# Four transformer layers: the residual in DRAM during the gate and up products, its tiles for the sums of weights

## The chip, the cores and the metric

One core of a Trainium2 chip. The metric is the device time of one execution in microseconds (us). Before: 2397.15 us, the median of 3 runs (2391.97 to 2398.90).

## The reference

Two blocks of two layers each, on 512 tokens of width 1024 in float32. Each layer is a mixer (several kinds of attention, convolution, gating), a projection back to the residual, and a feed-forward part of width 2816 with a gate. Cut to what the change touches:

```python
def first_block(x, ...):                 # layers 0 and 1
    for layer in range(2):
        mix = mixer(x, ...)
        x = layer_norm(ALPHA * x + mix, ln1_g, ln1_b)
        ffn = (silu(x @ w_gate) * (x @ w_up)) @ w_down
        x = layer_norm(ALPHA * x + ffn, ln2_g, ln2_b)

def second_block(x, ...):                # layers 2 and 3
    for l in range(2):
        x = x + rms_norm(mixer(rms_norm(x), ...) @ w_out, post)
        g, u = split(causal_dwconv(rms_norm(x) @ w_up, cw, cb), 2)
        x = x + rms_norm((gelu(g) * u) @ w_down, fpost)
```

In the feed-forward part the residual x is needed twice: normalized or as it is for the gate and up products, and again after the down product.

## The kernel before, in words

Tokens lie in four tiles of 128. The residual is four tiles `x` of 128 x 1024 float32. Every weight block of 512 KB is fetched by SyncE's queue into a tile `wraw` (three buffers) and split into a high part `whi` (ScalarE, line 248) and a low part `wlo` (VectorE, line 249). A product of a block is then three matmuls for each pair of parts, on TensorE (line 287).

The gate and up products of a layer (`quartered`, from line 514) run over 11 pieces u, each with four weight blocks b11, b12, b21, b22. For each piece the scheme makes seven products instead of eight, q1 to q7, of 24 matmuls each. Three of them take a block as it is: q1 takes b11, q2 takes b21, q3 takes b22. The other four take sums of blocks: q7 takes b12 + b22, q6 takes that + b11, q4 takes that + b21, q5 takes b11 + b12. The first three of these share one tile, `x` of the piece (tile `wsum`, three buffers), which grows from product to product; q5's sum lies in `t1` (tile `rope` or `m`, which hold gains of the normalization before and after).

Sums come about in two ways. GpSimd issues a transfer that adds a block from DRAM to the tile (line 632, 128 of them, and line 625, 8). VectorE adds two tiles (line 617 for t1 from piece 2 on, and line 630 for the last piece's q4: 40 in all). An addition to `wsum` can start only when the product before it has been split, for it changes the tile.

From piece 3 on the products come in the order q7(u), q4(u-1), q3(u-1), q6(u), q2(u), q5(u), q1(u+1); the code's order and the tiles' buffers set the order of work. The first pieces are mixed with the end of the out projection and the normalization: `add_norm` (layers 0 and 1) or `post` and `pre` (layers 2 and 3) finish one token tile after the other, and a function that waits in `self.later` turns each ("the crossing": transposes and sums of the operand's parts). Layers 0 and 1 finish a piece with silu and a multiplication (`gated`); layers 2 and 3 with a short convolution and gelu (`convolved`), which gives VectorE more work. After the products, `out_proj` makes the down product; it reads 22 weight blocks and then normalizes into the tiles `x`.

Of the kernel before, what the change touches and what calls it, by code (L numbers as in the profile page):

```python
# [9 lines left out]
F32 = mybir.dt.float32  # L10
F32R = mybir.dt.float32r
AF = mybir.ActivationFunctionType
ALU = mybir.AluOpType
# [3 lines left out]
P = 128  # L17
# [175 lines left out]
class Kernel:  # L193
# [58 lines left out]
            nc.vector.scalar_tensor_tensor(lo, src, scale, hi.bitcast(F32), op0=ALU.mult, op1=ALU.subtract)  # L252

    def raw(self):
        return self.tl("wraw", [P, 1024], F32, 3)

    def halves(self, place):

# [256 lines left out]
    def quartered(self, l, ops):  # L515
# [4 lines left out]

        nc, w = self.nc, self.t[f"up{l}"]
        room = self.room
        more = [self.piece() for _ in range(4)]
        at = lambda f: room[:, f] if f < 14 else more[f // 2 - 7][:, f % 2]
        sub = nc.vector.tensor_sub
        fc = self.small(f"fc{l}") if l >= 2 else None
        last = KF // 2 - 1

        def block(u, i, j):
            return w[u, i - 1, j - 1].rearrange("p g k c -> p (g k c)")
# [78 lines left out]
        def sums(u):  # L611

            s = st[u]
            s["x"] = load(u, 1, 2, self.tl("wsum", [P, 1024], F32, 3))
            if u > 1:
                first(u)
                nc.vector.tensor_tensor(s["t1"], s["b11"], s["x"], op=ALU.add)

        def first(u):

            s = st[u]
            s["t1"] = self.tl("rope" if u % 2 else "m", [P, D])
            if u < 2:
                load(u, 1, 2, s["t1"])
                nc.gpsimd.dma_start(s["t1"], block(u, 1, 1), accum_op=ALU.add)

        def added(u, i, j):
            x = st[u]["x"]
            if u == last and (i, j) == (2, 1):
                nc.vector.tensor_tensor(x, x, st[u]["b21"], op=ALU.add)  # L630
                return x
            nc.gpsimd.dma_start(x, block(u, i, j), accum_op=ALU.add)  # L632
            return x

        def q7(u):
            s = st[u]
            x = added(u, 2, 2) if u > 1 else s["x"]
            s["c"] = self.bank("tp")
            product(s["c"], x, 4, True)

        def q6(u):
            s = st[u]
# [19 lines left out]
            finish(2 * u, 1, None, (s["c"], s["m"]))  # L662

        sums(0)
        added(0, 2, 2)
        q1(0)
        sums(1)
        added(1, 2, 2)
        q2(0)
        q1(1)  # L670
        while self.later:
            self.behind(self.later.pop(0))
        q2(1)
        first(0)
        first(1)
        q1(2)
        q2(2)
        for f in (q7, 0), (q6, 0), (q7, 1), (q5, 0), (q6, 1), (q4, 0), (q5, 1), (q3, 0):
            f[0](f[1])
        for u in range(2, last + 1):  # L680
            if u == 2:
                sums(2)
            q7(u)
            q4(u - 1)
            q3(u - 1)
            q6(u)
            if u == 2:
                q1(3)
                sums(3)
                q5(2)  # L690
                continue
            q2(u)
            q5(u)
            if u < last:
                q1(u + 1)
                sums(u + 1)
        q3(last)
        q4(last)
        return at
# [668 lines left out]
    def add_norm(self, xs, l, which, nxt):  # L1368

        nc = self.nc  # L1370
        g, b = self.row(f"ln{which}_g", l, "rope"), self.row(f"ln{which}_b", l, "m")
        new = []

        def use(i, ps):
            v = xs[i]
            st = self.tl("lst", [P, 8], F32, 3)
            for j in range(2):
                h = slice(512 * j, 512 * j + 512)
                nc.vector.scalar_tensor_tensor(v[:, h], v[:, h], ALPHA, ps[j], op0=ALU.mult, op1=ALU.add,
                                               accum_out=st[:, j:j + 1])  # L1380
            nc.vector.tensor_scalar(st[:, 2:3], st[:, 0:1], st[:, 1:2], -1.0 / D, op0=ALU.add, op1=ALU.mult)
            nc.vector.tensor_scalar(st[:, 3:4], st[:, 2:3], 1.0 / 32, None, op0=ALU.mult)
            for j in range(2):
                junk = self.tl("rt", [P, S], F32, 2)
                nc.scalar.activation(junk, v[:, 512 * j:512 * j + 512], AF.Square, scale=1.0 / 32, bias=st[:, 3:4],  # L1385
                                     accum_out=st[:, 4 + j:5 + j])
            nc.vector.tensor_scalar(st[:, 6:7], st[:, 4:5], st[:, 5:6], LN_EPS, op0=ALU.add, op1=ALU.add)
            nc.gpsimd.tensor_tensor(st[:, 7:8], st[:, 6:7], self.mhalf[:, 0:1], op=ALU.pow)
            nc.vector.scalar_tensor_tensor(v, v, st[:, 2:3], g, op0=ALU.add, op1=ALU.mult)
            nc.vector.scalar_tensor_tensor(v, v, st[:, 7:8], b, op0=ALU.mult, op1=ALU.add)  # L1390
            new.append(v)
            return nxt(i, v)

        return use, new

    def pre(self, name, then, tag="m"):

# [17 lines left out]

        return use

    def post(self, xs, name, nxt, part=None):

        nc = self.nc  # L1420
        g = self.row(name, 0, "rope")

        def use(i, ps):
            yg = [self.tl("kf", [P, S], F32, 3) for _ in range(2)]
            cols = [slice(512 * j, 512 * j + 512) for j in range(2)]
            st = self.rstd(ps, lambda j: nc.vector.tensor_tensor(yg[j], ps[j], g[:, cols[j]], op=ALU.mult))
            for j, c in enumerate(cols):
                nc.vector.scalar_tensor_tensor(xs[i][:, c], yg[j], st[:, 3:4], xs[i][:, c], op0=ALU.mult, op1=ALU.add)
                if part:
                    part(i, xs[i], c)  # L1430
            return nxt(i, xs[i]) if nxt else None

        return use
# [5 lines left out]
    def run(self):  # L1439
        nc, t = self.nc, self.t  # L1440
        xt = self.parts()
        self.room = self.tl("room_a", [P, 14, S])
        raw = self.room[:, 0:8]

        idle = self.room[:, 13, 0:256]
        nc.vector.memset(idle, 0.0)
        ps = self.bank("sc")
        for _ in range(3):
            self.mm(ps[:, 0:256], idle[:, 0:P], idle)

        def start(k):
            steps = 1 if k else 2
            for i in range(steps):
                c = slice(i * S // steps, (i + 1) * S // steps)
                nc.sync.dma_start(raw[:, k, c], t["xT"][:, k, c])
                self.split(xt[0][:, k, c], xt[1][:, k, c], raw[:, k, c])

        self.start = start
        for l in range(2):
            y, order = self.mixer_a(xt) if l == 0 else self.mixer_c(xt)  # L1460
            if l == 0:
                xs = [self.tl("x", [P, D], F32, 4) for _ in range(NT)]
                for i in range(NT):
                    nc.sync.dma_start(xs[i], t["x"][P * i:P * i + P])
            ops = self.operands()
            use, new = self.add_norm(xs, l, 1, lambda i, v: lambda: self.crossed(v, i, ops))
            self.out_proj(lambda k: y[:, k], KD, t["a_out" if l == 0 else "c_out"], use, order, ops["parts"])
            xs = new
            if self.layers == l + 0.5:
                return [self.store(i, xs[i]) for i in range(NT)]  # L1470
            at = self.quartered(l, ops)
            xt = self.parts()
            last = self.layers == l + 1
            if l == 0:
                nxt = lambda i, v: lambda: self.transposed(v, i, xt)
            else:
                self.load_const("swap", "cmp_mask", "cmp_any", "pool_cnt")
                nxt = self.pre("pre2", lambda v, i: self.transposed(v, i, xt), "kf")
            use, new = self.add_norm(xs, l, 2, self.store if last else nxt)
            self.out_proj(at, KF, t[f"down{l}"], use, DOWN)  # L1480
            xs = new
            if last:
                return
        for l in (2, 3):
            y, order = self.mixer_n(xt, l)
            ops = self.operands()
            use = self.post(xs, f"post{l}", self.pre(f"fpre{l}", lambda v, i: self.crossed(v, i, ops)))
            self.out_proj(lambda k: y[:, k], KD, t[f"out{l}"], use, order, ops["parts"])
            if self.layers == l + 0.5:
                return [self.store(i, xs[i]) for i in range(NT)]  # L1490
            at = self.quartered(l, ops)
            last = self.layers == l + 1
            xt = None if last else self.parts()
            nxt = None if last else self.pre(f"pre{l + 1}", lambda v, i: self.transposed(v, i, xt))
            use = self.post(xs, f"fpost{l}", nxt, self.store if last else None)
            self.out_proj(at, KF, t[f"down{l}"], use, DOWN)
            if last:
                return
# [20 lines left out]
```

## Time and profile before

| | before |
|---|---|
| median of 3 runs | 2397.15 us (2391.97 to 2398.90) |
| the profiled execution | 2403.45 us, its span 2401.5 us |
| TensorE busy | 2284.9 us, 95% |
| VectorE busy | 1490.5 us, 62% |
| ScalarE busy | 1162.3 us, 48% |
| GpSimd busy | 187.1 us, 8% |
| mean granted TensorE clock | 0.979 of full speed |
| read from DRAM | 292.21 MB |

The profile is of one execution on the core's engines. A row's idle time is the time just before it in which its engine did nothing, with what ended it. The chain that ended last is followed back from the last instruction: each step is a piece of work or a transfer that released the next. The granted clock is what TensorE was allowed, as a share of 2.4 GHz. "Us to landing" of a transfer is the time from its issue to its arrival.

### The profile page before, as it was taken

What the parts mean: (1) busy time and instruction counts of PE and PEld (TensorE: products, weight loads), DVE (VectorE), ACT (ScalarE), POOL (GpSimd) and SP (SyncE); (2) the same over time, 40 slices, a digit from 0 to 9 for tenths busy, and PEclk for the clock granted to TensorE, in tenths of its full rate; (3) what the DMA queues carried; (4) which work ended last, traced back from release to release, by engine and by line L of the source; (5) the groups of instructions that cost most, each with busy time, mean ns of one, the idle gap of its engine ahead of it and who ended that gap; (6) DMA issues with size and microseconds to landing.
All of it is one profiled execution on the core that took longest, in us unless ns stands there. A gap on an engine that the chain in (4) does not pass through costs nothing.

```text
span 2401.5 us, 36736 instructions
## 1 busy us (share of the span) xinstructions
PE 2284.9 (95%) x14502; PEld 1966.6 (82%) x14502; DVE 1490.5 (62%) x2674; ACT 1162.3 (48%) x2079; POOL 187.1 (8%) x222
## 2 busy tenths in 40 slices
PE   9999799999999988999999998899999999889998
PEld 7668799988977778998888578899888758789987
DVE  4675556635365575655368667788546867678833
ACT  4574445523355544544343555667433365556732
POOL 1000111000000011110010001111000001111000
PEclk9999899999999999999999999999999999999999
DMA  7122777732333246775323217677432323667532
GB/s 213 49 82 94 163 171 190 203 97 75 95 109 97 71 107 149 197 193 153 115 78 101 83 53 167 137 189 197 125 105 82 105 72 99 139 160 188 136 105 71
DMA packets 94157, 301.01 MB, mean 125 GB/s; under 512 B 12952, under 2 KB 15896, under 8 KB 93984
## 3 DMA queue, kind: packets, MB, share of 16 engines
q1 hardware_dynamic: 74400, 227.35, 29.3%
q0 software_dynamic: 19584, 71.31, 17.2%
q8 instruction: 114, 1.87, 0.3%
q14 instruction: 59, 0.48, 0.1%
HBM read 292.21 MB, written 2.11 MB: 123 GB/s over the span
## 4 chain that ended last, share of the span: by engine, by line
PE 65%; DMA 11%; DVE 11%; issue 7%; ACT 4%; POOL 1%; SPq 0%; DVEq 0%; POOLq 0%; ACTq 0%
PE mm L287 21%; PE sc L287 20%; PE tp L287 13%; DMA wsum<-in_up 10%; PE o L287 8%; DVE wlo L249 3%; PE tp L769 2%; DVE q L582 2%; ACT whi L248 1%; DVE xl L249 1%; ACT rt L406 1%; POOL pst L416 1%; ACT rt L1385 0%; DVE pr L1413 0%; DVE pr L738 0%
## 5 line engine op out<-in xcount | busy, mean ns | idle before, releaser
L249 DVE TENSOR_TENSOR wlo<-wraw,whi 128x1024 fp32r<-128x1024 f32 (+5 forms) x325 | 377.0, 1162 | 425.8 <-ACT whi L248 420.5
L248 ACT CAST whi<-wraw 128x1024 fp32r<-128x1024 f32 (+4 forms) x323 | 323.6, 1005 | 553.1 <-PE sc L287 354.1
L287 PE MATMUL mm<-xh,whi 128*128 128x256 f32 (+1 forms) x1040 | 323.0, 311 | 5.7 <-DVE room_a L803 3.1
L287 PE MATMUL mm<-xh,wlo 128*128 128x256 f32 (+1 forms) x1040 | 320.6, 309 | 0.0
L287 PE MATMUL mm<-xl,whi 128*128 128x256 f32 (+1 forms) x1040 | 319.3, 307 | 1.0 <-DVE xl L249 1.0
L249 DVE TENSOR_TENSOR wlo<-wsum,whi 128x1024 fp32r<-128x1024 f32 x132 | 160.5, 1221 | 163.2 <-ACT whi L248 158.7
L248 ACT CAST whi<-wsum 128x1024 fp32r<-128x1024 f32 x132 | 138.1, 1050 | 239.0 <-DMA wsum<-in_up 167.8
L287 PE MATMUL sc<-pr,whi 128*128 128x256 f32 x704 | 198.9, 283 | 25.6 <-ACT whi L248 13.0
L287 PEld LDWEIGHTS mm<-xh,whi 128*128 128x128 f32 x1040 | 197.8, 190 | 22.9 <-issue 8.3
L287 PEld LDWEIGHTS mm<-xh,wlo 128*128 128x128 f32 x1040 | 197.1, 190 | 12.9 <-issue 2.6
L287 PEld LDWEIGHTS mm<-xl,whi 128*128 128x128 f32 x1040 | 197.8, 190 | 11.5 <-DVE xl L249 1.2
L287 PE MATMUL sc<-pr,wlo 128*128 128x256 f32 x704 | 197.7, 281 | 4.3 <-DVE wlo L249 4.2
L632 POOL DMA_DIRECT2D wsum<-in_up x128 | 111.7, 881 | 758.2 <-DVE wlo L249 441.8
L287 PEld LDWEIGHTS sc<-pr,whi 128*128 128x128 f32 x704 | 135.0, 192 | 28.5 <-ACT whi L248 14.3
L287 PEld LDWEIGHTS sc<-pr,wlo 128*128 128x128 f32 x704 | 134.4, 191 | 6.2 <-DVE wlo L249 6.1
L287 PE MATMUL tp<-xh,whi 128*128 128x256 f32 x400 | 117.1, 293 | 11.9 <-DVE rt L556 10.7
L287 PE MATMUL sc<-xh,whi 128*128 128x256 f32 x352 | 102.2, 290 | 22.5 <-ACT kf L645 22.4
L754 ACT ACTIVATE pr<-pr,mx 128x512 f32<-128x512 f32 (+3 forms) x160 | 88.3, 555 | 69.4 <-DVE mx L752 69.4
L287 PE MATMUL tp<-xl,whi 128*128 128x256 f32 x400 | 115.3, 288 | 0.0
L287 PE MATMUL tp<-xh,wlo 128*128 128x256 f32 x400 | 115.0, 287 | 0.0
L287 PE MATMUL tp<-pr,whi 128*128 128x256 f32 x352 | 100.2, 285 | 11.5 <-ACT whi L248 11.5
L287 PE MATMUL tp<-pr,wlo 128*128 128x256 f32 x352 | 99.8, 283 | 1.1 <-DVE wlo L249 0.9
(493 smaller groups left out, 5834.6 us busy)
## 6 DMA issues: line engine op xcount, KB each, us to landing
wraw<-in_up SPq DMA_DIRECT2D x132, 512.0 KB, 5.0
wsum<-in_up POOLq DMA_DIRECT2D x128, 512.0 KB, 6.4
wraw<-in_down SPq DMA_DIRECT2D x88, 512.0 KB, 3.6
wsum<-in_up SPq DMA_DIRECT2D x44, 512.0 KB, 6.9
wraw<-in_i_fm SPq DMA_DIRECT2D x20, 512.0 KB, 3.7
wraw<-in_c_fm SPq DMA_DIRECT2D x16, 512.0 KB, 3.5
wraw<-in_out SPq DMA_DIRECT2D x16, 512.0 KB, 3.6
wraw<-in_i_tok SPq DMA_DIRECT2D x16, 326.0 KB, 2.8
```

The source lines that it names most:

```text
L248: nc.scalar.copy(hi, src)
L249: nc.vector.tensor_sub(lo, src, hi.bitcast(F32))
L287: self.last_mm = self.nc.tensor.matmul(out, a, b, start=start, stop=stop, **k)
L406: self.nc.scalar.activation(junk[:, :n], src, AF.Square, scale=scale, accum_out=dst)
L416: self.nc.gpsimd.tensor_tensor(st[:, 3:4], st[:, 2:3], self.mhalf[:, 0:1], op=ALU.pow)
L582: nc.vector.scalar_tensor_tensor(o[:, i:], raw[j][:, :S - i], wt(2 - i), o[:, i:], op0=ALU.mult, op1=ALU.add)
L632: nc.gpsimd.dma_start(x, block(u, i, j), accum_op=ALU.add)
L754: nc.scalar.activation(prt[t], prt[t], AF.Exp, bias=mx[:, 1, t:t + 1], scale=scale, accum_out=mx[:, 2, t:t + 1])
L769: nc.tensor.transpose(ps[:, at:at + P], prt[t][:, P * kt:P * kt + P], self.ident)
```

## The change

Between the normalization after the mixer and the down product, the residual is not kept in its four tiles. Each tile is written to DRAM as soon as it is final (`spill`, 4 stores of 512 KB for each layer), and is read back before the down product (`restored`, 4 loads). In between, the four tiles `x` hold the sums of weights: x of every piece, and t1 of pieces 0 and 1. The tiles `wsum` are gone, and `wraw` has six buffers for three.

In layers 0 and 1 VectorE makes all sums (44 for each layer). In layers 2 and 3 the first sums of a piece, t1 and b12 + b22, are made by GpSimd's adding transfers into tiles that no product reads yet, and VectorE adds b11 and b21 (22 for each layer). In all VectorE's additions go from 40 to 132 and the adding transfers from 136 to 44. For pieces 0 to 2 the blocks to be added are loaded once more; SyncE's loads of these weights go from 184 to 250. The order of the products on TensorE stays.

```diff
     def raw(self):
-        return self.tl("wraw", [P, 1024], F32, 3)
+        return self.tl("wraw", [P, 1024], F32, 6)
...
-        sub = nc.vector.tensor_sub
+        sub, add = nc.vector.tensor_sub, lambda o, a, b: nc.vector.tensor_tensor(o, a, b, op=ALU.add)
...
         def sums(u):
             s = st[u]
-            s["x"] = load(u, 1, 2, self.tl("wsum", [P, 1024], F32, 3))
-            if u > 1:
-                first(u)
-                nc.vector.tensor_tensor(s["t1"], s["b11"], s["x"], op=ALU.add)
-
-        def first(u):
-            s = st[u]
-            s["t1"] = self.tl("rope" if u % 2 else "m", [P, D])
-            if u < 2:
-                load(u, 1, 2, s["t1"])
-                nc.gpsimd.dma_start(s["t1"], block(u, 1, 1), accum_op=ALU.add)
+            s["x"] = load(u, 1, 2, self.tl("x", [P, D], F32, 4))
+            s["t1"] = self.tl("x", [P, D], F32, 4) if u < 2 else self.tl("rope" if u % 2 else "m", [P, D])
+            if l < 2:
+                b11 = load(u, 1, 1) if u < 3 else s["b11"]
+                add(s["t1"], b11, s["x"])
+                add(s["x"], s["x"], load(u, 2, 2))
+            else:
+                load(u, 1, 1, s["t1"])
+                nc.gpsimd.dma_start(s["t1"], block(u, 1, 2), accum_op=ALU.add)
+                nc.gpsimd.dma_start(s["x"], block(u, 2, 2), accum_op=ALU.add)
 
         def added(u, i, j):
             x = st[u]["x"]
-            if u == last and (i, j) == (2, 1):
-                nc.vector.tensor_tensor(x, x, st[u]["b21"], op=ALU.add)
-                return x
-            nc.gpsimd.dma_start(x, block(u, i, j), accum_op=ALU.add)
+            add(x, x, load(u, i, j) if u < 3 else st[u]["b%d%d" % (i, j)])
             return x
 
         def q7(u):
             s = st[u]
-            x = added(u, 2, 2) if u > 1 else s["x"]
             s["c"] = self.bank("tp")
-            product(s["c"], x, 4, True)
+            product(s["c"], s["x"], 4, True)
...
         sums(0)
-        added(0, 2, 2)
         q1(0)
-        sums(1)
-        added(1, 2, 2)
         q2(0)
...
         q2(1)
-        first(0)
-        first(1)
+        sums(1)
         q1(2)
         q2(2)
...
+        sums(2)
         for u in range(2, last + 1):
-            if u == 2:
-                sums(2)
             q7(u)
             q4(u - 1)
             q3(u - 1)
             q6(u)
-            if u == 2:
-                q1(3)
-                sums(3)
-                q5(2)
-                continue
-            q2(u)
-            q5(u)
+            if u > 2:
+                q2(u)
+                q5(u)
             if u < last:
                 q1(u + 1)
                 sums(u + 1)
+            if u == 2:
+                q5(u)
...
     def add_norm(self, xs, l, which, nxt):
...
+            if which == 1:
+                self.spill(i, v)
             return nxt(i, v)
...
+    def spill(self, i, v):
+        if i == 0:
+            self.kept = self.tc.dram_tile([NT, P, D], F32, name=f"kept_{self.n}")
+        self.nc.sync.dma_start(self.kept[i], v)
+
+    def restored(self):
+        xs = [self.tl("x", [P, D], F32, 4) for _ in range(NT)]
+        for i in range(NT):
+            self.nc.sync.dma_start(xs[i], self.kept[i])
+        return xs
...
-    def post(self, xs, name, nxt, part=None):
+    def post(self, xs, name, nxt, part=None, spill=False):
...
+            if spill:
+                self.spill(i, xs[i])
             return nxt(i, xs[i]) if nxt else None
...
             at = self.quartered(l, ops)
+            xs = self.restored()
```

`run` passes `spill=True` to `post` of layers 2 and 3, and calls `restored` after `quartered` in all four.

What this does to the order of instructions shows at three places. First, VectorE in layer 0's normalization after the mixer, between the token tiles 2 (`x_1646`) and 3 (`x_1647`); L1379 and L1390 are the first sum and the last step of a tile. Before:

```order
L249 TENSOR_TENSOR xl_1653<-tp_1964,xh_1652 128x4x128
L1382 TENSOR_SCALAR lst_1946<-lst_1946 128x1
L1379 SCALAR_TENSOR_TENSOR x_1647,lst_1999<-x_1647,sc_1664 128x512
L1387 TENSOR_SCALAR lst_1946<-lst_1946 128x1
L1389 SCALAR_TENSOR_TENSOR x_1646<-x_1646,lst_1946,rope_1654 128x1024
L1390 SCALAR_TENSOR_TENSOR x_1646<-x_1646,lst_1946,m_1656 128x1024
L1379 SCALAR_TENSOR_TENSOR x_1647,lst_1999<-x_1647,sc_1665 128x512
```

With the change (L1368 and L1379 are those lines now, L529 is an addition of weights; `x_2057` is x of piece 0, in the place of token tile 0, and `x_2059` its t1, in the place of tile 1):

```order
L249 TENSOR_TENSOR xl_1653<-tp_1970,xh_1652 128x4x128
L1371 TENSOR_SCALAR lst_1951<-lst_1951 128x1
L529 TENSOR_TENSOR x_2059<-wraw_2060,x_2057 128x1024
L1368 SCALAR_TENSOR_TENSOR x_1647,lst_2005<-x_1647,sc_1664 128x512
L1376 TENSOR_SCALAR lst_1951<-lst_1951 128x1
L1378 SCALAR_TENSOR_TENSOR x_1646<-x_1646,lst_1951,rope_1654 128x1024
L1368 SCALAR_TENSOR_TENSOR x_1647,lst_2005<-x_1647,sc_1665 128x512
L1379 SCALAR_TENSOR_TENSOR x_1646<-x_1646,lst_1951,m_1656 128x1024
L1370 TENSOR_SCALAR lst_2005<-lst_2005 128x1
L529 TENSOR_TENSOR x_2057<-x_2057,wraw_2063 128x1024
```

The two additions of piece 0's sums have moved in between the steps of tile 2's and tile 3's normalization.

Second, GpSimd in layer 2's normalization, where L416 is the power that gives 1/sqrt for one token tile (twice for each tile). Before:

```order
L416 TENSOR_TENSOR pst_13063<-pst_13063,mhalf 128x1
L416 TENSOR_TENSOR pst_13074<-pst_13074,mhalf 128x1
L416 TENSOR_TENSOR pst_13127<-pst_13127,mhalf 128x1
L416 TENSOR_TENSOR pst_13138<-pst_13138,mhalf 128x1
L416 TENSOR_TENSOR pst_13190<-pst_13190,mhalf 128x1
L625 DMA rope_13422<-in_up 128x1024
L416 TENSOR_TENSOR pst_13201<-pst_13201,mhalf 128x1
```

With the change (L625 adds b22 to x of pieces 0 and 1, L624 adds b12 to t1 of piece 0):

```order
L416 TENSOR_TENSOR pst_13131<-pst_13131,mhalf 128x1
L416 TENSOR_TENSOR pst_13167<-pst_13167,mhalf 128x1
L625 DMA x_13358<-in_up 128x1024
L416 TENSOR_TENSOR pst_13179<-pst_13179,mhalf 128x1
L416 TENSOR_TENSOR pst_13232<-pst_13232,mhalf 128x1
L624 DMA x_13360<-in_up 128x1024
L416 TENSOR_TENSOR pst_13244<-pst_13244,mhalf 128x1
L416 TENSOR_TENSOR pst_13296<-pst_13296,mhalf 128x1
L625 DMA x_13526<-in_up 128x1024
```

Three adding transfers, into the places of the token tiles 0, 1 and 2, now stand between the powers, where one stood, into `rope`.

Third, SyncE's queue at the same place of layer 0. Before:

```order
L536 DMA wraw_2123<-in_up 128x1024
L536 DMA wraw_2185<-in_up 128x1024
L536 DMA wraw_2224<-in_up 128x1024
L536 DMA wraw_2258<-in_up 128x1024
L536 DMA wraw_2512<-in_up 128x1024
L536 DMA rope_2221<-in_up 128x1024
L536 DMA m_2218<-in_up 128x1024
L536 DMA wraw_2612<-in_up 128x1024
```

With the change:

```order
L538 DMA wraw_2234<-in_up 128x1024
L1391 DMA kept_1870<-x_1644 128x1024
L538 DMA x_2057<-in_up 128x1024
L1391 DMA kept_1870<-x_1645 128x1024
L538 DMA wraw_2237<-in_up 128x1024
L1391 DMA kept_1870<-x_1646 128x1024
L538 DMA wraw_2271<-in_up 128x1024
L538 DMA wraw_2333<-in_up 128x1024
L538 DMA x_2228<-in_up 128x1024
L1391 DMA kept_1870<-x_1647 128x1024
```

The spills of the four token tiles (L1391) have come in between the loads, and a load into a tile `x` stands behind the spill of what it held.

## Rows read from the trace of the kernel before

**Rows 1.** page, parts 1 and 4: busy time by engine; the chain by line

```profile
PE 2284.9 (95%) x14502; PEld 1966.6 (82%) x14502; DVE 1490.5 (62%) x2674; ACT 1162.3 (48%) x2079; POOL 187.1 (8%) x222
...
PE mm L287 21%; PE sc L287 20%; PE tp L287 13%; DMA wsum<-in_up 10%; PE o L287 8%; DVE wlo L249 3%; PE tp L769 2%; DVE q L582 2%; ACT whi L248 1%; DVE xl L249 1%; ACT rt L406 1%; POOL pst L416 1%; ACT rt L1385 0%; DVE pr L1413 0%; DVE pr L738 0%
```

**Rows 2.** windows by stage: span, busy PE PEld DVE ACT POOL, granted clock, DMA share, GB/s

```profile
251.48:332.71 81.23, 67.31 (x530) 66.18 (x529) 41.93 (x49) 32.59 (x45) 10.52 (x12) 0.89 0.65 144
332.71:446.95 114.24, 114.24 (x1010) 114.24 (x1009) 71.73 (x83) 59.90 (x84) 15.84 (x18) 1.00 0.82 203
446.95:470.51 23.56, 23.56 (x201) 23.03 (x200) 17.84 (x24) 14.44 (x22) 0.88 (x1) 1.00 0.67 202
878.50:960.68 82.18, 66.85 (x530) 65.91 (x529) 41.56 (x49) 32.56 (x45) 10.41 (x12) 0.90 0.63 141
960.68:1074.92 114.24, 114.24 (x1010) 114.24 (x1009) 69.79 (x80) 57.16 (x80) 15.70 (x18) 1.00 0.81 201
1074.92:1104.34 29.42, 26.71 (x201) 25.99 (x200) 19.84 (x26) 17.00 (x26) 0.86 (x1) 0.88 0.64 185
1457.37:1539.19 81.82, 67.71 (x529) 64.99 (x527) 56.72 (x76) 43.84 (x64) 10.52 (x13) 0.93 0.66 145
1539.19:1663.60 124.41, 118.87 (x1008) 117.00 (x1009) 102.98 (x132) 82.56 (x122) 16.53 (x19) 0.98 0.75 186
1663.60:1691.38 27.78, 25.71 (x202) 24.68 (x200) 22.89 (x33) 18.36 (x30) 0.86 (x1) 0.94 0.69 190
2039.78:2124.62 84.84, 66.68 (x530) 63.83 (x528) 56.53 (x76) 43.95 (x64) 10.40 (x12) 0.94 0.65 141
2124.62:2248.04 123.42, 119.09 (x1009) 117.62 (x1010) 103.24 (x132) 82.80 (x122) 15.62 (x18) 0.97 0.73 178
2248.04:2275.97 27.93, 25.56 (x202) 24.71 (x200) 22.52 (x31) 18.16 (x29) 0.00 (x0) 0.94 0.39 114
```

**Rows 3.** chain that ended last, layer 0's start-up: start, us, what

```profile
248.19 7.39 DMA wsum<-in_up
...
259.34 7.01 DMA wsum<-in_up
...
302.87 8.48 DMA wsum<-in_up
...
324.71 2.72 PE mm L287 x24
```

**Rows 4.** the same chain, layer 1's tail and layer 2's steady stage

```profile
1062.68 13.31 DMA wsum<-in_up
...
1586.42 7.34 DMA wsum<-in_up
```

**Rows 5.** instructions of line 617: duration ns min/median/max, first and last start

```profile
L617 DVE TENSOR_TENSOR m<-wraw,wsum x20: 1209/1222/1226, 261.0 to 2227.9; 128x1024 f32<-128x1024 f32 x20
```

**Rows 6.** page, part 6: DMA issues, us to landing; last line: tile out's eight stores

```profile
wraw<-in_up SPq DMA_DIRECT2D x132, 512.0 KB, 5.0
wsum<-in_up POOLq DMA_DIRECT2D x128, 512.0 KB, 6.4
...
DMA to landing us min/median/max: 2.0/2.0/4.1
```

**Rows 7.** timeline of VectorE, layer 0's normalization: start, us, instruction, idle before

```profile
222.11 1.28 DVE L1390 SCALAR_TENSOR_TENSOR x<-x,lst,m 128x1024 f32<-128x1024 f32 x1
...
227.10 0.69 DVE L1379 SCALAR_TENSOR_TENSOR x<-x,sc 128x512 f32<-128x512 f32 x1 [0.87 <-PE sc L287]
```

**Rows 8.** timelines of VectorE and GpSimd, layer 2's normalization

```profile
1422.22 1.42 DVE L1428 SCALAR_TENSOR_TENSOR x<-kf,pst,x 128x512 f32<-128x512 f32 x2 [0.73 <-POOL pst L416]
...
1431.48 0.55 POOL L416 TENSOR_TENSOR pst<-pst,mhalf 128x1 f32<-128x1 f32 x1 [2.66 <-DVE pst L415]
```

**Rows 9.** timeline of VectorE, the opening of the program

```profile
41.95 0.17 DVE L1272 TENSOR_SCALAR ch<-s_cv 128x4 f32<-128x4 f32 x1 [3.71 <-DMA s_cv<-in_cv]
```

More of the change, by code (lines that the diff above doesn't have):

```diff
@@ L1486, in run @@
             ops = self.operands()
-            use = self.post(xs, f"post{l}", self.pre(f"fpre{l}", lambda v, i: self.crossed(v, i, ops)))
+            use = self.post(xs, f"post{l}", self.pre(f"fpre{l}", lambda v, i: self.crossed(v, i, ops)), spill=True)
             self.out_proj(lambda k: y[:, k], KD, t[f"out{l}"], use, order, ops["parts"])
@@ L1491, in run @@
             at = self.quartered(l, ops)
+            xs = self.restored()
             last = self.layers == l + 1
```

## The prediction

> **What bounds the kernel now.** The page first. TensorE is busy for 95% of the span and VectorE for 62% [rows 1], so by the shares nothing but TensorE matters. The chain that ended last says otherwise: 10% of the span, some 240 us, is a wait for `wsum<-in_up`, the transfers that fetch the weight sums and add to them. A share cannot tell where they hurt, so I cut the gate and up products of the four layers into stages [rows 2]: start-up (first matmul of q7(0) to that of q7(4)), steady (to q7(10)) and tail (to the end of the products). One product is 24 matmuls and takes 2.72 us at full clock [rows 3]. The start-up holds 22 products (four of q7, q6 and q5, three of q4 and q3, two of q1 and q2), so 22 x 2.72 = 59.8 us is its floor; it takes 81.2, 82.2, 81.8 and 84.8 us. The steady stage holds 42, floor 114.24 us, and layers 0 and 1 sit on that floor to the hundredth; layers 2 and 3 take 124.4 and 123.4 us. The tail takes 23.6 us in layer 0 and 29.4, 27.8 and 27.9 us in the others. Summed against floor (the tail against layer 0's): start-ups lose 21.4 + 22.4 + 22.0 + 25.0, steady stages 10.2 + 9.2, tails 5.9 + 4.2 + 4.4, in all 125 us. That is all that this change can win in these stages. The same rows show that part of it is clock: granted 0.89 to 0.94 of the 2.4 GHz in the start-ups, 1.00 where TensorE is never idle.
>
> The chain says what those losses wait for [rows 3]: in layer 0's start-up 7.4, 7.0 and 8.5 us on `wsum` transfers, one behind another, since one tile is filled for q7, then added to for q6, then for q4, and each addition can start only when VectorE has read the tile for the product before. In layer 1's tail one such transfer took 13.3 us, and in layer 2's steady stage 7.3 us stands in the middle of VectorE's work [rows 4].
>
> **The change part by part.**
>
> *Sums by VectorE.* An addition of two weight blocks costs 1.222 us [rows 5]. Additions go from 40 to 132, that is 92 x 1.22 = 112 us more on VectorE. What they replace in layers 0 and 1 is an addition transfer of 6.4 us median from its issue to landing [rows 6], behind the same release. Does VectorE have room? Layer 0's start-up: 41.9 us busy [rows 2], and 12 more additions (16 for 4, counted in the order of the two programs), 41.9 + 12 x 1.22 = 56.6 us, under the 59.8 us floor. Layers 0 and 1, steady: 71.7 us plus at most 24 more additions (four for each of six pieces) is 101 us, under 114.2. Layer 2's start-up: 56.7 + 3 x 1.22 = 60.4 us against 59.8, full. Its steady stage: 103.0 + 7 x 1.22 = 111.5 us against 114.2, 98% full. So layers 0 and 1 can come near the floor, layers 2 and 3 cannot quite.
>
> *The weights come earlier.* Six `wraw` buffers for three let SyncE fetch two pieces ahead, but the first pieces are bound to the residual's slots: x of piece 0 goes into tile 0's slot, t1 into tile 1's, and so on. x of pieces 2 and 3 waits for slots that VectorE frees four rows before it adds to them, a transfer of 5.0 us [rows 6] against some 3 us of other rows: 2 us each, 4 in all. I keep 3 us for bank drains, so start-ups in layers 0 and 1 go to 59.8 + 7.2 = 67 us. In layers 2 and 3 a filled VectorE and the addition transfer for piece 2, which comes 2 to 5 us late, make it 70.
>
> *The spill.* Four stores of 512 KB for each layer, on SyncE's queue. No row shows such a store. Bounds: the 256 KB output stores land in 2.0 us [rows 6], and the slowest 512 KB transfer took 13.3 [rows 4]. I take 4 us, twice the store of half the size, which is the nearest row. What waits for it: in layer 0 VectorE has the addition into tile 1's slot between two parts of the normalization. Tile 1 is final at 222.1 + 1.3 = 223.4 us, so its slot is free at 227.4, while VectorE went on to tile 3 at 227.1 after a short idle time of 0.9 us [rows 7]: some 1 us of wait and 1.2 us of work, less what the idle time takes up, 2 us for each of layers 0 and 1. In layer 2, GpSimd has the addition transfer for tile 0's slot ahead of the power that tile 1's second normalization waits for. Tile 0 is final at 1423.6 us; plus 4 (spill) plus 5 (load) is 1432.6, where the power stood at 1431.5 [rows 8]: 1.1 us late and 0.6 us of issue, and the same once more at tile 2, 3.5 us for each of layers 2 and 3. The rule for the sum: each further microsecond of spill costs about 10, two in each of layers 0 and 1, three in each of layers 2 and 3.
>
> The Trainium skill, "DMA: Bandwidth & Descriptors", section on the anatomy of one DMA on the gpsimd path, gives 2.0 us plus bytes over 436 GB/s; by that 512 KB is an estimate of 3.2 us, and the sum would be 8 us better. The same section warns that the completion of a write to HBM can be "a surprisingly long delay", which speaks against this change. The 2.0 us of the 256 KB stores do not show it.
>
> *The reload.* Four loads for each layer, placed among the last weight loads and the first six of the down product. The last waits for q4(10)'s parts; six down blocks lie ahead of it, and nobody reads the tile before the down product ends, so I put it at nothing. Were that cover gone, it would cost one load, 5 us a layer.
>
> *Steady and tail.* In layers 2 and 3 the wait for the transfers goes and one addition per piece comes: 118 us against 124.4 and 123.4, between the floor and now, since VectorE has 2.7 us to spare. Layer 1's tail loses its 13.3 us transfer and comes to 25 us; layers 2 and 3 win 1.3 and 1.4 there, a third of their loss, as VectorE is nearly full.
>
> *The opening.* VectorE waits 3.7 us for a small constant [rows 9] which stands on SyncE's queue behind layer 0's first sums. These loads are now made late, so I count 3 us won.
>
> **The sum.** Start-ups 12 (81.2 to 67 + 2), 13, 8 (81.8 to 70 + 3.5) and 11; steady 6.4 + 5.4; tails 4.4 + 1.3 + 1.4; opening 3: 66 us. The profiled execution took 2403.45 us, which gives 2337.5. It lay 6 us above the median of the runs, 2397.15, so against that the forecast is 2331 us. Its own range is a gain of 45 to 90, 2307 to 2352.
>
> **The rivals.**
>
> *VectorE becomes the bound.* For: its demand in layers 2 and 3 is 98 to 101% of the floor, its rows run in a fixed order, and each row that waits for a slot holds all behind it. Against: layers 0 and 1 have room. Then start-ups of layers 2 and 3 and both steady stages win nothing, those of layers 0 and 1 win half, 6 each; with tails 7.1 and opening 3 that is 22 us: 2375 us.
>
> *Near the floor.* For: layers 0 and 1's steady stages show that the order of products can run without a gap. Start-ups of 63 us in layers 0 and 1 and 65 in 2 and 3 (18.2 + 19.2 + 16.8 + 19.8 = 74), steady 116 (7.4 to 8.4 each), tails 7 and opening 3: 100 us, 2297 us.
>
> *Slower: the spill lands late.* All first sums hang on it, and VectorE or GpSimd stands still in mid-normalization, so that the crossing and then TensorE wait. A spill of 4 + D us costs two waits less 2 us of slack each in layers 0 and 1, 2D - 4, and three in layers 2 and 3, 3D: 10D - 8 in all. It eats the 66 us, and is slower by more than can be measured, from D = 8, a spill of 12 us; at the 13.3 us bound it is 85 against 66, 2416 us. Against: queues are 63 to 66% busy there and stores were quick.
>
> *No change.* The waits only change their name: SyncE loads 250 weight blocks where it loaded 184, and with fewer additions and the 32 spills and reloads the bytes stay nearly what they were (326 transfers of 512 KB for 320), so if arrival of weights sets the pace, nothing is won: 2397 us. Against: three of four waits in the chain are for additions, not for first loads.
>
> **How the numbers follow.** Forecast 0.50, near the floor 0.17, VectorE bound 0.20, no change 0.06, slower 0.07. The range 2293 to 2381 us takes in the first three with a few microseconds about the outer ones, leaving out the last two and their edges, some 0.15. A run of this kernel can tell 0.3%, 7 us, from no change. Faster than that 0.87 (the first three), same 0.06, slower 0.07.
>
> **What would show it.** In the new profile, right: start-ups of 65 to 75 us at a granted clock of 0.95 or more, steady stages of layers 0 and 1 still at 114.24, the waits for sums nearly gone from the chain; spills landing in 3 to 5 us. VectorE bound: the chain in layers 2 and 3 runs through VectorE's rows without idle time and a piece stays at 19.5 us or more. Late spill: VectorE's `x` addition or GpSimd's power shows idle time released by the store, and TensorE idles ahead of q7(0). I am wrong altogether if layers 0 and 1 lose their floor in the steady stage, for then additions stand in front of the parts TensorE needs next, or if the last reload makes the down product wait.

## The result, and the profile after

The changed kernel took 2329.11 us (median of 4 runs, 2323.90 to 2334.69), the kernel before 2398.03 us in the same rounds: a ratio of 0.9708, 95% interval 0.9665 to 0.9752. That is 69 us faster; the forecast was 66 us, to 2331 us. Later rounds put the same gain at 72 and 83 us (the experiments below), so how near the forecast came is partly luck of the round. The profiled execution of the changed kernel took 2334.69 us, its span is 2332.9 us, 68.6 us under the span before.

The page of the changed kernel, parts 1, 4 and 6, against [rows 1, 6]:

```profile
PE 2270.3 (97%) x14502; PEld 1961.0 (84%) x14502; DVE 1596.9 (68%) x2766; ACT 1165.7 (50%) x2079; POOL 106.8 (5%) x130
...
PE sc L287 28%; PE mm L287 26%; PE tp L287 17%; PE o L287 8%; DVE wlo L249 2%; PE tp L758 2%; DMA x<-in_up 1%; ACT whi L248 1%; DVE q L584 1%; POOL pst L416 1%; DVE pr L1416 1%; DVE xl L249 1%; DVE x L529 1%; ACT rt L406 0%; DVE pr L727 0%
...
wraw<-in_up SPq DMA_DIRECT2D x184, 512.0 KB, 4.1
...
x<-in_up POOLq DMA_DIRECT2D x26, 512.0 KB, 7.3
kept<-x SPq DMA_DIRECT2D x16, 512.0 KB, 2.6
```

VectorE has 106 us more to do (1490.5 to 1596.9; the count gave 112), and the wait for sums went from 10% of the chain to 1% (`x<-in_up`). The spills land in 2.6 us (the median of 16; the slowest took 4.5).

The stages of [rows 2], same columns, for the changed kernel (start-up, steady and tail of layers 0, 1, 2, 3):

```profile
241.59:314.87 73.28, 66.76 (x551) 65.97 (x551) 64.16 (x71) 34.69 (x49) 0.00 (x0) 0.95 0.60 191
314.87:433.59 118.72, 118.72 (x1011) 118.72 (x1009) 92.75 (x101) 60.02 (x84) 0.00 (x0) 1.00 0.44 134
433.59:457.89 24.30, 24.30 (x202) 23.77 (x201) 16.80 (x23) 14.46 (x23) 0.00 (x0) 1.00 0.50 157
859.33:932.83 73.50, 66.78 (x550) 65.99 (x551) 64.15 (x71) 34.70 (x49) 0.00 (x0) 0.95 0.60 189
932.83:1051.55 118.72, 118.72 (x1010) 118.72 (x1009) 92.75 (x101) 60.02 (x84) 0.00 (x0) 1.00 0.44 134
1051.55:1075.86 24.31, 24.31 (x202) 23.78 (x201) 16.81 (x23) 14.46 (x23) 0.00 (x0) 1.00 0.57 180
1430.14:1497.06 66.92, 60.50 (x486) 59.12 (x484) 56.06 (x74) 42.67 (x61) 7.63 (x9) 0.95 0.81 208
1497.06:1617.67 120.61, 119.62 (x1054) 119.41 (x1053) 117.40 (x147) 85.66 (x126) 8.65 (x10) 1.00 0.69 184
1617.67:1642.08 24.41, 23.92 (x202) 23.07 (x200) 22.62 (x32) 18.36 (x29) 0.00 (x0) 1.00 0.60 193
1991.58:2057.76 66.18, 59.44 (x485) 57.70 (x483) 56.10 (x74) 42.64 (x61) 7.92 (x9) 0.95 0.80 208
2057.76:2183.04 125.28, 124.28 (x1054) 124.07 (x1053) 118.90 (x149) 85.92 (x126) 8.78 (x10) 1.00 0.67 179
2183.04:2207.50 24.46, 24.29 (x201) 23.64 (x200) 22.22 (x29) 18.36 (x29) 0.00 (x0) 1.00 0.50 165
```

Two warnings on reading this beside the rows before. In layers 2 and 3 q7(4) now sends its first matmuls ahead, among those of other products, so their border lies earlier (1054 matmuls in the steady window where 42 products are 1008); start-up and steady are best added there. And q7(0) itself comes at another place in its layer, so I also count from the first matmul of q1(0): 229.62, 856.06, 1440.70 and 2023.11 us before, 224.87, 842.57, 1411.88 and 1973.23 after.

| term | forecast, us | profiled execution, us |
|---|---|---|
| start-up, layer 0 and 1 (from q1(0)) | 12 + 13 | 13.1 + 14.4 |
| steady, layer 0 and 1 | 0 | -4.5 - 4.5 |
| start-up and steady, layer 2 and 3 (from q1(0)) | 14.4 + 16.4 | 17.1 + 15.1 |
| tails, layers 0 to 3 | 0 + 4.4 + 1.3 + 1.4 | -0.7 + 5.1 + 3.4 + 3.5 |
| opening, to q1(0) | 3 | 4.7 |
| all the rest | 0 | 1.9 |
| sum | 66 | 68.6 |

Where it still waits: TensorE's timeline, one place in layer 0 (layer 1 alike), one in layer 2 (layer 3: 4.93 us), and then ScalarE's ahead of the second:

```profile
247.74 0.58 PE L287 MATMUL mm<-xh,wlo 128*128 128x256 f32 x1 [4.68 <-DVE wlo L249]
...
1456.17 0.58 PE L287 MATMUL sc<-xh,whi 128*128 128x256 f32 x1 [5.25 <-ACT kf L641]
...
1454.59 1.04 ACT L248 CAST whi<-x 128x1024 fp32r<-128x1024 f32 x1 [8.41 <-DMA x<-in_up]
1455.54 0.58 ACT L641 COPY kf<-sc 128x512 f32<-128x512 f32 x1
```

The first is VectorE: between 218 and 257 us it has little idle time, and the low part that TensorE wants stands behind the crossing and four additions. The second is x of piece 2: its load and then its adding transfer into a slot that came free late; ScalarE's `whi` waits 8.41 us for it, and the copy `kf`, which empties the bank that q5 needs, stands behind that `whi`.

### The profile page after: what moved, and what is told of

The parts are those of the page before. It is cut to its first block, busy times and chain, and to the rows that moved or that the text cites. A ratio compares the mean times of both kernels' runs of the same rounds, so it can differ in the third digit from the quotient of the medians.

```text
span 2332.9 us, 36844 instructions
## 1 busy us (share of the span) xinstructions
PE 2270.3 (97%) x14502; PEld 1961.0 (84%) x14502; DVE 1596.9 (68%) x2766; ACT 1165.7 (50%) x2079; POOL 106.8 (5%) x130
## 4 chain that ended last, share of the span: by engine, by line
PE 82%; DVE 9%; ACT 3%; issue 2%; DMA 2%; POOL 1%; DVEq 0%; POOLq 0%; SPq 0%; ACTq 0%
PE sc L287 28%; PE mm L287 26%; PE tp L287 17%; PE o L287 8%; DVE wlo L249 2%; PE tp L758 2%; DMA x<-in_up 1%; ACT whi L248 1%; DVE q L584 1%; POOL pst L416 1%; DVE pr L1416 1%; DVE xl L249 1%; DVE x L529 1%; ACT rt L406 0%; DVE pr L727 0%
## 5 line engine op out<-in xcount | busy, mean ns | idle before, releaser
L248 ACT CAST whi<-x 128x1024 fp32r<-128x1024 f32 x140 | 146.6, 1050 | 140.2 <-PE mm L287 55.3
L287 PEld LDWEIGHTS mm<-xh,whi 128*128 128x128 f32 x1040 | 199.1, 192 | 16.7 <-issue 4.8
L249 DVE TENSOR_TENSOR wlo<-x,whi 128x1024 fp32r<-128x1024 f32 x140 | 170.2, 1220 | 49.0 <-ACT whi L248 48.5
L529 DVE TENSOR_TENSOR x<-x,wraw 128x1024 f32<-128x1024 f32 x110 | 134.1, 1221 | 1.8
L743 ACT ACTIVATE pr<-pr,mx 128x512 f32<-128x512 f32 (+3 forms) x160 | 88.3, 555 | 69.8 <-DVE mx L741 69.8
L287 PE MATMUL sc<-xh,wlo 128*128 128x256 f32 x352 | 100.3, 285 | 2.0 <-DVE wlo L249 2.0
L287 PE MATMUL tp<-pt,whi 128*128 128x256 f32 x352 | 98.8, 281 | 1.5 <-DVE pt L249 1.4
```

The lines of the kernel that those rows point to most:

```text
L248: nc.scalar.copy(hi, src)
L249: nc.vector.tensor_sub(lo, src, hi.bitcast(F32))
L287: self.last_mm = self.nc.tensor.matmul(out, a, b, start=start, stop=stop, **k)
L529: sub, add = nc.vector.tensor_sub, lambda o, a, b: nc.vector.tensor_tensor(o, a, b, op=ALU.add)
L743: nc.scalar.activation(prt[t], prt[t], AF.Exp, bias=mx[:, 1, t:t + 1], scale=scale, accum_out=mx[:, 2, t:t + 1])
```

## The experiments

Each ran beside the kernel before in the same rounds; ratios are against that. Where the intervals of two kernels overlap, their times alone do not tell them apart, and only the lengths of stages in the profiles can.

**The changed kernel again** (no edit).

> The changed kernel, once more. Its gate and up products ran at two paces at the same granted clock of 1.00: 2.72 us for a product in layer 2's steady stage (114.2 us for 42 products), 2.83 us in those of layers 0, 1 and 3 (118.7 us). If the program sets the pace, the same three stages are slow again and the span lies within 3 us of 2332.9. If the pace is drawn at each restart of TensorE, other stages are slow, and the span moves by some 4.5 us for each stage that changes: 2315 to 2336 us.

It took 2325.89 us (2316.82 to 2332.34), ratio 0.9684, 0.9651 to 0.9718; the profiled span is 2315.0 us, 17.9 us under the first one. All steady stages ran at the faster pace. The 10 us from 400 us on, first in the first profile, then in the second, and below it the second profile's steady stage of layer 0:

```profile
400.00:410.00 10.00, 10.00 (x87) 10.00 (x86) 9.04 (x10) 5.37 (x8) 0.00 (x0) 1.00 0.36 107
```

```profile
400.00:410.00 10.00, 10.00 (x91) 10.00 (x90) 7.71 (x8) 6.25 (x9) 0.00 (x0) 1.00 0.61 174
...
312.85:427.09 114.24, 114.24 (x1010) 114.24 (x1009) 92.73 (x101) 60.00 (x84) 0.00 (x0) 1.00 0.46 140
```

TensorE is busy without a gap in all three, the granted clock is 1.00, and yet 87 matmuls lie wholly or partly in the 10 us of the first profile and 91 in those of the second (118.72 or 114.24 us for the 1008 of a steady stage: 117.8 or 113.3 ns each). So the pace isn't set by the program: the same program draws it anew. It accounts for most of the 17.9 us: from q1(0) to the last product the first execution is longer by 6.3 us in layer 0, and its three steady stages at the slower pace alone hold some 4.5 us each.

**The sums without the spill.**

```diff
-        return self.tl("wraw", [P, 1024], F32, 6)
+        return self.tl("wraw", [P, 1024], F32, 4)
...
-            s["x"] = load(u, 1, 2, self.tl("x", [P, D], F32, 4))
-            s["t1"] = self.tl("x", [P, D], F32, 4) if u < 2 else self.tl("rope" if u % 2 else "m", [P, D])
+            s["x"] = load(u, 1, 2, self.tl("wsum", [P, D], F32, 2))
+            s["t1"] = self.tl("rope" if u % 2 else "m", [P, D])
```

and no calls of `spill` and `restored`.

> The changed kernel's sums without its spill: the residual stays in its tiles, x of a piece lies in two tiles wsum, t1 always in rope and m, wraw has 4 buffers (six tiles in all, as in both kernels). Theory that the freed tiles carry the gain of the start-up: the first sums wait for rope and m and for two wsum tiles, start-ups go back by 5 to 10 us each and the later pieces lose some, 2355 to 2385 us. Rival, that VectorE's additions in place of the transfers carry it and the spill buys nothing: 2322 to 2338 us.

2338.78 us (2336.32 to 2353.12), ratio 0.9753, 0.9717 to 0.9789: just above the rival's band and well below the theory's. From q1(0) the start-ups of layers 0 and 1 are 93.0 and 95.8 us where the second profile of the changed kernel has 88.9 and 88.6, and q1(0) to q7(10) of layers 2 and 3 is 209.5 and 209.8 us where it has 204.7 and 206.6. So the spill and the two more `wraw` buffers that its tiles pay for buy some 13 us of the 72 (2338.78 against 2325.89, in the same rounds; the intervals of the two ratios only just touch). Four fifths of the gain come without them, from how the sums are made.

**All additions by transfers, with the spill.**

```diff
-            if l < 2:
+            if l < 0:
                 b11 = load(u, 1, 1) if u < 3 else s["b11"]
...
-            add(x, x, load(u, i, j) if u < 3 else st[u]["b%d%d" % (i, j)])
+            nc.gpsimd.dma_start(x, block(u, i, j), accum_op=ALU.add)
```

> The changed kernel's tiles and spill, but every addition made by a GpSimd transfer as before (none by VectorE). Theory that the chain of transfers into one tile was the loss: start-ups from q7(0) go back to 75 to 82 us, steady stages of layers 2 and 3 to 120 to 124, 2370 to 2400 us. Rival, that buffers that come free early carry the gain: 2325 to 2345 us. VectorE has 132 additions less, 161 us of busy time; if VectorE were the bound anywhere in the changed kernel, that stage gets shorter here.

2482.03 us (2478.79 to 2484.62), ratio 1.0337, 1.0313 to 1.0360: 84 us slower than before, worse than the theory's band and far from the rival's. Its page, parts 5 and 6, and its steady stage of layer 0:

```profile
L248 ACT CAST whi<-x 128x1024 fp32r<-128x1024 f32 x140 | 145.7, 1049 | 392.6 <-DMA x<-in_up 343.3
...
x<-in_up POOLq DMA_DIRECT2D x140, 512.0 KB, 7.5
```

```profile
328.15:466.26 138.11, 125.50 (x1010) 123.19 (x1009) 65.58 (x79) 58.43 (x84) 18.37 (x21) 0.94 0.80 199
```

ScalarE waits 343 us for adding transfers, and even the steady stage of layer 0 leaves its floor. The kernel before had 136 such transfers plus 40 additions by VectorE, this one has 176. So it is more than an undoing of the change, and it can't give VectorE's additions a price; but it answers the rival: six `wraw` buffers and the residual's tiles don't help when each sum is a chain of transfers of 7.5 us.

**Each tile stored four times.**

```diff
         self.nc.sync.dma_start(self.kept[i], v)
+        for j in range(3):
+            self.nc.sync.dma_start(self.more[i, j], v)
```

> The changed kernel with each residual tile stored four times (three copies that nobody reads), so that a tile comes free some 3 to 6 us later than after one store of 2.6 us. By the rule of the prediction, 10 us for each microsecond less the slack of 8, this costs 22 to 52 us: 2350 to 2380 us, with VectorE or GpSimd idle in mid-normalization. Rival, that the slots have slack: within 8 us of the changed kernel, 2322 to 2340 us.

2337.39 us (2330.83 to 2341.55), ratio 0.9737, 0.9704 to 0.9769: 11.5 us more than the changed kernel in the same rounds, with intervals that overlap. That is well below the theory's band; the time lies inside the rival's 2322 to 2340, the difference outside its 8 us. From q1(0) to q7(4) layers 0 and 1 take 88.3 and 86.1 us, no longer than the 88.9 and 88.6 of one store; from q1(0) to q7(10) layers 2 and 3 take 211.9 and 213.2 us for 204.7 and 206.6. The three copies land in 4.7 us median. GpSimd's timeline in layer 2 shows that more than the landing changed:

```profile
1403.35 1.37 POOL L416 TENSOR_TENSOR pst<-pst,mhalf 128x1 f32<-128x1 f32 x1 [4.07 <-DVE pst L415]
1408.16 0.55 POOL L416 TENSOR_TENSOR pst<-pst,mhalf 128x1 f32<-128x1 f32 x1 [3.45 <-DVE pst L415]
1408.92 1.05 POOL L625 DMA_DIRECT2D x<-in_up  x1 [0.21 <-issue]
1419.46 0.88 POOL L624 DMA_DIRECT2D x<-in_up  x1 [9.49 <-DMA x<-in_up]
```

With four stores in the program the order is another: all powers of the normalization come first, and the first adding transfer after them, at 1408.92 us, where the second profile of the changed kernel has it at 1389.81. So this run prices a spill that is late and known to be late; one that is late in an order which doesn't expect it was not tried.

**Layers 2 and 3 by VectorE too** (`if l < 4` for `if l < 2` in `sums`).

> VectorE makes all sums in layers 2 and 3 too (44 additions for each layer instead of 22, the same in all four layers; no GpSimd transfers). Theory that VectorE is nearly full there: one piece gets 2 x 1.22 us more on 18.1 of 19.04, so 20.3 us or more for a piece, steady stages 120.6 to 128 or more each (from q7(4)'s first matmul), 2335 to 2355 us. Rival, that VectorE still has room and the transfers cost more than they save: 2305 to 2325 us.

2342.38 us (2336.47 to 2344.72), ratio 0.9743, 0.9715 to 0.9771, in the theory's band. Steady stages of layers 2 and 3:

```profile
1498.59:1619.18 120.59, 117.78 (x1010) 115.84 (x1009) 120.55 (x148) 80.92 (x120) 0.00 (x0) 1.00 0.41 132
2067.80:2188.29 120.49, 117.54 (x1010) 115.74 (x1009) 120.46 (x150) 81.69 (x120) 0.00 (x0) 1.00 0.39 130
```

VectorE is busy 120.55 of 120.59 us for 42 products, 20.1 us a piece against a floor of 19.04. From q1(0) the start-ups also grow, to 93 us from 84 to 86. So in layers 2 and 3 VectorE has room for two additions in a piece, and not for four.

**Piece 2 and 3 of layers 2 and 3 by VectorE.**

```diff
-                nc.gpsimd.dma_start(s["x"], block(u, 2, 2), accum_op=ALU.add)
+                if u in (2, 3):
+                    add(s["x"], s["x"], load(u, 2, 2))
+                else:
+                    nc.gpsimd.dma_start(s["x"], block(u, 2, 2), accum_op=ALU.add)
```

> In layers 2 and 3 alone, b22 of pieces 2 and 3 is added by VectorE from a loaded block, not by GpSimd's transfer. Theory that the 4.7 to 5.3 us in which TensorE idles for kf in these start-ups come from the load and then the adding transfer into a slot that comes free late: that idle time falls to under 2.5 us, 3 us less for each of layers 2 and 3. Rival, that VectorE is full in the start-up: the idle time moves to another row and the two stages keep their sum of 204 to 207 us from q1(0) to q7(10).

2323.02 us (2310.80 to 2327.01), ratio 0.9657, 0.9620 to 0.9695. The idle time for `kf` is gone; an idle time for a low part is left near that place, 2.89 us in layer 2 (not under 2.5, as expected) and 1.81 in layer 3:

```profile
1438.52 0.38 PE L287 MATMUL sc<-pr,wlo 128*128 128x256 f32 x1 [2.89 <-DVE wlo L249]
```

From q1(0) to q7(10) layers 2 and 3 take 202.3 and 200.5 us, 2.4 and 6.1 less than in the second profile of the changed kernel. The time alone doesn't show it: the interval overlaps the changed kernel's 0.9651 to 0.9718.

**Piece 1's sums later in layers 0 and 1** (`sums(1)` after `q2(2)`).

> In layers 0 and 1 alone, piece 1's sums are written after q2(2) instead of before q1(2). Theory that the 4.7 us in which TensorE idles for wlo ahead of q7(0) are VectorE's crowded crossing, with two additions of piece 1 in it: that idle time falls by about 2.3 us, and start-ups from q1(0) go from 88.9 and 88.6 to 86.5. Rival, that the additions only move to where they delay q7(1): no change in the start-up (88 to 90).

2322.64 us (2314.99 to 2329.41), ratio 0.9664, 0.9626 to 0.9701. The idle time of 4.68 us is 2.12 us, and the start-ups from q1(0) are 86.43 and 86.51 us, as expected. The time alone shows nothing here either: the span, 2327.7 us, holds three steady stages at the slower pace.

**First sums by transfers in layers 0 and 1.**

```diff
-            if l < 2:
+            if l < 2 and u > 1:
                 b11 = load(u, 1, 1) if u < 3 else s["b11"]
```

> In layers 0 and 1 the first sums of pieces 0 and 1 (t1 and b12 + b22) are made by GpSimd's transfers as in layers 2 and 3, four additions of VectorE fewer in the crossing. Theory that VectorE's row there is the limit: start-ups from q1(0) 84 to 87 us (88.9 and 88.6 with the change). Rival, that the transfers hold GpSimd's power of the normalization: q1(0) starts 2 us later or more, and the start-up is 88 to 95.

2315.65 us (2310.60 to 2321.63), ratio 0.9628, 0.9595 to 0.9662. q1(0) of layer 0 starts at 223.89 us, no later, and its start-up takes 82.6 us (layer 1: 84.1). From q7(0) to q7(4):

```profile
244.51:306.44 61.93, 61.93 (x530) 61.68 (x529) 56.80 (x63) 33.21 (x46) 0.86 (x1) 1.00 0.65 202
```

22 products in 61.9 us, TensorE without a gap, granted clock 1.00: the floor at the slower pace (22 x 2.83 = 62.2), with a few products at the faster one. The transfers stand between GpSimd's powers here too, but they cost VectorE nothing in the crossing.

**Both together, and the changed kernel beside it.**

> The two edits that shortened a stage, together: in layers 0 and 1 the first sums of pieces 0 and 1 by GpSimd's transfers, in layers 2 and 3 b22 of pieces 2 and 3 added by VectorE. They touch different layers, so their gains should add: layers 0 and 1 from q1(0) to q7(4) 82 to 85 us, layers 2 and 3 from q1(0) to q7(10) 200 to 203, 2303 to 2315 us by the pace that TensorE draws. Rival, that they share a queue or a cover: 2316 us or more, like the better one alone.

> The changed kernel beside it, in the same rounds: 2322 to 2332 us. The pace is drawn again: with all long stretches at 2.72 us for a product the span is near 2315, with all at 2.83 near 2335.

Both edits: 2298.87 us (2297.33 to 2308.42), ratio 0.9566, 0.9544 to 0.9588; the changed kernel in the same rounds 2322.61 us (2319.69 to 2328.92), ratio 0.9657, 0.9635 to 0.9679. The edits add: layers 0 and 1 from q1(0) to q7(4) in 82.7 and 83.1 us (90.4 and 89.8 in the changed kernel beside it), layers 2 and 3 from q1(0) to q7(10) in 202.2 and 203.0 (206.7 and 205.7), the time below the expected band. It beats both kernels, by 24 us and by 107 us. The changed kernel beside it ran every steady stage at the faster pace, and yet its profiled span is 2320.5 us, 5.5 above the second profile's: the pace of the steady stages is not the whole of the spread.

**Four wraw buffers** (4 for 6).

> The changed kernel with four wraw buffers for six. Theory that the first sums are bound by the tiles x and by VectorE, not by wraw: within 6 us, 2320 to 2336. Rival, that blocks held for the additions (b11 until q6, b21 until q4) fill four buffers and hold the loads: steady stages of layers 0 and 1 leave their floor, 2340 us or more.

2329.55 us (2323.70 to 2335.91), ratio 0.9691, 0.9666 to 0.9716, 7 us above the changed kernel in the same rounds, one more than expected, with intervals that overlap. Steady stages of layers 0 and 1 are 114.24 us, so the rival is out. The buffers above four carry little: the 7 us are not clear of noise.

## Why the prediction was right

**The bound and the floor** held. The waits that the chain named were the ones that went, and the clock came with them: 0.89 to 0.94 in the start-ups before, 0.95 now.

**Sums by VectorE** were the main term, and the runs say so more strongly than the text: without the spill 59 of 72 us remain, without any addition by VectorE (the 40 of the kernel before included) all is lost and 84 us more. VectorE's room in the steady stages was read rightly: layers 0 and 1 keep TensorE without a gap with 92.75 us of VectorE in the steady stage (bound given: 101), and layers 2 and 3 stand at the brink (117.4 of 120.6 us busy), over which two more additions a piece push them. In layer 0's start-up it was not: the sum gave VectorE 56.6 us there, under the floor of 59.8, and it was busy 64.16 of 73.28 us, 21.2 of them in additions. That window takes in most of the last product ahead of q7(0), which explains a part.

**Steady stages of layers 2 and 3** were forecast at 118 us. From the bulk of q7(4) at 1503.65 us layer 2 takes 114.0, the floor, and so do layers 2 and 3 in the second profile:

```profile
1503.65:1617.67 114.02, 114.02 (x1009) 114.02 (x1007) 110.81 (x139) 82.96 (x121) 7.79 (x9) 1.00 0.71 190
```

A VectorE that is 97% busy cost nothing there, so the term was too small by some 4 us a layer.

**The steady stage of layers 0 and 1** was to stay at 114.24 us; in the profiled execution it took 118.72, and I had said that I would then be wrong altogether, since additions would stand in front of parts that TensorE needs. The step that failed is that reading: TensorE has no idle time in these windows, and the repeated kernel shows 114.24. It is a pace, not a wait.

**The spill** landed in 2.6 us by the median (4 taken), the slowest in 4.5. The Trainium skill, "DMA: Bandwidth & Descriptors", section on the anatomy of one DMA on the gpsimd path, gave an estimate of 3.2 us, nearer than my 4 and still above the median; it is for GpSimd's path, and the spills went by SyncE's queue. Its warning of a long completion does not show. My wait of 1 us at tile 1's slot came in layer 1 only, where the store took 3.4 us and VectorE idled 0.71 us for it; in layer 0 VectorE ran the addition without idle time (timeline of the changed kernel, layer 0, then layer 1):

```profile
221.40 1.23 DVE L529 TENSOR_TENSOR x<-wraw,x 128x1024 f32<-128x1024 f32 x1
222.54 0.68 DVE L1368 SCALAR_TENSOR_TENSOR x<-x,sc 128x512 f32<-128x512 f32 x1
...
839.89 1.22 DVE L529 TENSOR_TENSOR x<-wraw,x 128x1024 f32<-128x1024 f32 x1 [0.71 <-DMA kept<-x]
```

Of the 3.5 us that I took for each of layers 2 and 3, at most 1.7 show: q1(0) starts no later after the products of the layer before (336.0 and 331.2 us, 336.4 and 331.7 before the change), and q7(0) follows it after 18.3 and 18.4 us for 16.7.

**The price of a late spill**, 10 us for each microsecond, is not shown: four stores, two microseconds later by the median landing (4.7 for 2.6) and up to four by the slowest copy (6.6), cost 11.5 us, and the stages that got longer are those of layers 2 and 3. Layers 0 and 1 have slack, as the rival's sum had it (2 us each). But the order reacts to the stores, so the 11.5 us are the price of another order too, and neither 10 nor a smaller price follows from them.

**The 4 us for slot-bound loads** were right in kind in layers 2 and 3, where piece 2's x cost 5.25 and 4.93 us of TensorE; the edit that replaced its transfer won 2.4 and 6.1. In layers 0 and 1 it was another thing that cost as much: VectorE's own additions in the crossing, which I had counted as 1.2 us of work and which cost 4.68 us of TensorE ahead of q7(0). Moving two of them took away 2.6; with all four as transfers that idle time is gone.

**Tails** won 11.3 us for 7.1, since layers 2 and 3 came down to 24.4 and not by a third. **The opening** won 4.7 us for 3: the idle time of 3.7 us is gone [rows 9], and with it the low clock beside it, which I had not counted. The 10 us from 40 us on, before and after:

```profile
40.00:50.00 10.00, 7.21 (x19) 5.72 (x20) 5.60 (x15) 2.50 (x9) 3.71 (x5) 0.66 0.53 138
```

```profile
40.00:50.00 10.00, 10.00 (x47) 7.53 (x46) 8.21 (x19) 5.27 (x16) 4.70 (x8) 1.00 0.41 117
```

So the sum met the result partly by errors that cancel: 9 us lost to the pace in layers 0 and 1, some 8 us won beyond the forecast in tails, opening and the rest.

## What to carry to other kernels

Look at the wait for each fill of a buffer before its share: stages with a chain of adding transfers of 6 to 8 us each into one tile stood 125 us above their floor, and 106 us more of work on an engine with idle time, with the spill, took more than half of that away. Choose per stage who makes a sum: where VectorE is crowded (normalization, heavy gates) a transfer into a tile that nobody reads yet is better, where a slot comes free late an addition of 1.2 us beats a transfer of 7 us. Before a stage that got longer is explained, count its idle time: if there is none, and it holds the same work at the same granted clock, run it again.

## What the runs showed of the hardware

At a granted clock of 1.00 and without a gap, the same matmuls ran at 113.3 ns or at 117.8 ns each, mostly for a whole stage at a time; the same program drew either in different executions. It moves this kernel by up to 4.5 us for each steady stage, about 0.2% of its time, and what selects it stays open: no run here settles that.

A 512 KB store to DRAM landed in 2.6 us, sooner than loads of the same size into `wraw` (4.1 us) in the same kernel, and an adding transfer in 7.3 us, nearly twice such a load; all three are medians.
